# Tile places in SBUF: an identity, two padded buffers and a smaller constant in a one-core encoder kernel

## The chip, the core and the metric

The kernel runs on one core of a Trainium2 chip. TensorE (PE in the profile, with its weight loads as PEld) multiplies, VectorE (DVE), ScalarE (ACT) and GpSimd (POOL) do the elementwise work, and SyncE (SP) issues most transfers. Each engine works through its own list of instructions and waits for the others through semaphores. Operands lie in SBUF, a memory of 128 partitions; a tile has the same byte address in every partition. Products are written to PSUM. The metric is the device time of one execution in microseconds (us).

## What is computed

One layer of a hybrid encoder over 1024 positions of 1024 channels, all in float32:

```python
h = layer_norm(x, emb_ln_g, emb_ln_b)
proj = h @ w_in
q, k, v, z_a, u, z_b, g_a, g_b = split(proj)
attn = neighbourhood_attention(q, k, v, rpb)          # 8 heads of 64
y_a = attn * silu(z_a)
u = centred_depthwise_conv(u, conv_w, conv_b)         # 4 taps
hh = rg_lru(u, gates of direction 0) + rg_lru(u, gates of direction 1, reverse=True)
y_b = hh * silu(z_b)
m = sigmoid(g_a + b_merge[0]) * (y_a @ w_ba) + sigmoid(g_b + b_merge[1]) * (y_b @ w_bb)
out = layer_norm(ALPHA * h + m @ w_out, ln_g, ln_b)
```

In `rg_lru` the gates are `sigmoid(x_block @ w_gate + b_gate)`, with blocks of 64 channels, followed by a linear scan along the sequence.

## The kernel before

**Arithmetic.** A float32 operand is split into a high and a low part of the type fp32r, and a product becomes three: high by high, low by high, high by low (`mm3`, whose matmul is line 134). In `PE.matmul(o, a, b)` the operand `a` is stationary (loaded into the array by a weight load of 128 columns) and `b` is moving (streamed through it, up to 512 columns). The projection and the output product use a Strassen-like scheme of seven products of half size.

**Stages.** First the embedding layer norm, transposes of h and the projections of v and of half of q (to about 82 us). Then 17 pairs of output columns, seven products each (`slot` counts them), and between these, hung into the slots by `at(...)`, the recurrent branch: `take_u` copies u into a padded buffer `up`, `conv_stage` forms four taps from it and splits the result into `us`, and `gate_stage` multiplies `us` by the gate weights `gw` and scans. Then attention (about 430 to 532 us), with the products of the LRU branch as filler, and last the merge and the output product with its layer norm.

**Order.** The instructions of every engine run in the order in which the code issues them (a manual schedule is entered before the first load), and semaphores hold back what isn't ready. Only the few instructions on the constants at the head of the function, the identity among them, stand ahead of that schedule.

**Places.** Pools are stacked, some from the bottom of the partition ("left"), some from the top ("right"), and a tile's size is rounded up to 32 bytes. The pool `cst` is the first one on the left; the six tiles in it are, in the order of their allocation, ident (512 bytes), eps_t, eps_z (4 bytes each), smh (240), warm (4) and sm (240). It starts at byte 640, and the pool `hb` with the high and low parts of h follows it, then `wsp` with the weight parts and `hts`. On the right, `ev` ends the region of `lru` at byte 212960; `lru` holds sp, nsp, three small tiles, us0, us1, r, two buffers up, i, two uc, gw high and low, a and two wh.

**The identity** `ident` is built by `make_identity` with two GpSimd instructions, a memset and an affine select. It is the moving operand of every transpose: of gb_row and gb_col (lines 415 and 213), of the layer-norm tiles x (line 272), of the probabilities p (line 1130) and of the row sums (line 1175). The stationary operand is the data that is transposed.

**The gate products** are issued in `gate_stage`, at line 806: for each of four channel blocks t, two directions d, two halves b and two column halves n, a group of two matmuls, `gw` high and low against the same `us`. That makes 64 matmuls of 512 columns. `us` holds the high part in 64 partitions and the low part in the other 64.

**The halved constants** `smh` are 0.5 times all of `sm`, written once in `decay_rates` (line 651). They are read as a bias by `take_zg` (line 702), and only its columns from `SM_BM` (44) on, the sixteen merge biases, are used.

Of the kernel before, what the change touches and what calls it, by code (L numbers as in the profile page):

```python
# [10 lines left out]
F32 = mybir.dt.float32  # L11
F32R = mybir.dt.float32r
AF = mybir.ActivationFunctionType
ALU = mybir.AluOpType

P = 128
S = 1024
# [29 lines left out]
SM_CW, SM_CB, SM_GB, SM_LAM, SM_BM, SM_N = 0, 16, 20, 36, 44, 60  # L47
# [9 lines left out]
def tiled(ap, n):  # L57

    return ap[:, n * HALF:(n + 1) * HALF].rearrange("p (j r c) -> p j r c", r=GR, c=8)


def gridded(ap, n):

    return ap.rearrange("p (r j c) -> p j r c", r=GR, c=8)[:, 4 * n:4 * n + 4]
# [3 lines left out]
def encoder_kernel(ctx, tc, x, gb1, gb, w_qk, w_v, w_s, w_ba, w_bb, w_gate, smalls, bias, w_out, out):  # L68
    nc = tc.nc
    V, A, G, PE, SP = nc.vector, nc.scalar, nc.gpsimd, nc.tensor, nc.sync  # L70

    def pool(name, side="left", **kw):
        return tc.alloc_tile_pool(name=name, bufs=1, side=side, reuse_waits="tile", **kw)
# [5 lines left out]
    cst = pool("cst")  # L79
# [23 lines left out]
    ga_d = dram.tile([NK, P, S], F32, name="ga_d")  # L103
    gb_d = dram.tile([NK, P, S], F32, name="gb_d")

    ident = cst.tile([P, P], F32, name="ident")
    make_identity(nc, ident[:])
    eps_t = cst.tile([P, 1], F32, name="eps_t")
    V.memset(eps_t[:], EPS)
    eps_z = cst.tile([P, 1], F32, name="eps_z")  # L110
    V.memset(eps_z[:], EPS * TWICE * TWICE)
    smh = cst.tile([P, SM_N], F32, name="smh")
    warm = cst.tile([P, 1], F32, name="warm")
    A.activation(warm[:], eps_t[:], AF.Sqrt)
    sm = cst.tile([P, SM_N], F32, name="sm")

# [527 lines left out]
    lru = pool("lru", "right")  # L644
# [3 lines left out]
    lam = sm[:, SM_LAM:SM_LAM + 8]  # L648

    def decay_rates():  # L650
        V.tensor_scalar(smh[:], sm[:], 0.5, None, ALU.mult)
        V.tensor_scalar(t0[:], lam, -1.0, None, ALU.mult)
        V.tensor_tensor(t0[:], lam, t0[:], ALU.min)
        A.activation(t0[:], t0[:], AF.Exp)
        yield
        V.tensor_scalar(t1[:], t0[:], 2.0, None, ALU.add)
        V.reciprocal(t1[:], t1[:])
        V.tensor_tensor(t0[:], t0[:], t1[:], ALU.mult)
        V.tensor_tensor(t1[:], t0[:], t0[:], ALU.mult)
        V.tensor_scalar(t2[:], t1[:], 1.0 / 21.0, 1.0 / 19.0, ALU.mult, ALU.add)  # L660
        yield
        for n in (17, 15, 13, 11, 9, 7, 5, 3, 1):
            V.tensor_tensor(t2[:], t2[:], t1[:], ALU.mult)
            V.tensor_scalar(t2[:], t2[:], 1.0 / n, None, ALU.add)
            if n in (13, 7, 1):
                yield
        V.tensor_tensor(t2[:], t2[:], t0[:], ALU.mult)
        V.tensor_scalar(t0[:], lam, -1.0, 0.0, ALU.mult, ALU.max)
        V.scalar_tensor_tensor(t0[:], t2[:], 2.0, t0[:], ALU.mult, ALU.add)
        V.tensor_scalar(sp[:], t0[:], C_LRU, None, ALU.mult)  # L670
        V.tensor_scalar(nsp[:], t0[:], -C_LRU, None, ALU.mult)
        yield
# [2 lines left out]

    def take_u(m0):
        for m in (m0, m0 + 1):
            up = lru.tile([P, S + 3], F32, tag="up", bufs=2, name=f"up{m}")
            V.memset(up[:, 0:2], 0.0)
            V.memset(up[:, S + 2:S + 3], 0.0)  # L680
            ups[m] = up

        def consume(mi, n, add, o):
            dst = gridded(ups[m0 + mi][:, 2:2 + S], n)
            if add is None:
                A.copy(dst, tiled(o[:], 0))
            else:
                V.tensor_tensor(dst, tiled(add[:], 0), tiled(o[:], 0), ALU.add)
            return []
        return consume  # L690

    def take_zg(dst, m0, name, col=None):

        def consume(mi, n, add, o, c=None):
            c = o if c is None else c
            if add is not None:
                V.tensor_tensor(c[:], add[:], o[:], ALU.add)
            z = ev.tile([P, HALF], F32, tag="z", bufs=5, name=f"{name}{m0}{mi}{n}")

            def squash():  # L700
                bias = {} if col is None else dict(bias=smh[:, col + m0 + mi:col + m0 + mi + 1])
                A.activation(z[:], c[:], AF.Tanh, scale=0.5, **bias)

            def store():
                if col is None:
                    V.scalar_tensor_tensor(z[:], z[:], 1.0, c[:], ALU.add, ALU.mult)
                SP.dma_start(dst[m0 + mi][:, n * HALF:(n + 1) * HALF], z[:])
            return [squash, store]
        return consume
# [233 lines left out]
            load_k(h)  # L943

    def gates_a(j):
        return lambda: take_zg(ga_d, 2 * j, "ga", SM_BM)

    def gates_b(j):
        return lambda: take_zg(gb_d, 2 * j, "gb", SM_BM + 8)

    takes = [take_q, lambda: take_u(0), lambda: take_zg(zb_d, 0, "zb"), lambda: take_zg(za_d, 0, "za"), gates_a(0), gates_a(1),
             lambda: take_u(2), gates_b(0), lambda: take_zg(zb_d, 2, "zb"), gates_a(2), gates_b(1),
             lambda: take_k(0), gates_a(3), lambda: take_k(2), lambda: take_zg(za_d, 2, "za"), gates_b(2), gates_b(3)]
    rates = decay_rates()
    for slot in range(8, 14):
        at(slot, 1, lambda: next(rates))
# [427 lines left out]
    for slot in range(16):  # L1384
        j, n = divmod(slot, 2)
# [234 lines left out]
    for slot in range(16 + len(plan)):  # L1620
        j, n = divmod(slot, 2)
# [142 lines left out]
```

## Time and profile before

| | |
|---|---|
| median of 3 runs | 663.64 us (663.38 to 663.95) |
| the profiled execution's own time | 663.47 us |
| its span, first to last instruction | 661.7 us |
| mean granted TensorE clock | 0.997 |
| matmuls and weight loads | 3119 each |

The profile is of one execution. Its span leaves out 1.77 us around the first and the last instruction. In a row of a group, the number behind "x" is the count, then come the busy time in us, the mean length of one instruction in ns, and the idle time of its engine just before. A matmul's length in the trace is longer than its distance to the next one, since matmuls overlap in the array: a product of 512 columns is shown with 389 ns and the next one starts some 228 ns after it. A view of a tile gives the lowest, median and highest length, and the start of the first and of the last instruction. A row of the timeline begins with the start in us and the length in us of the run of instructions.

### The profile page before, as it was taken

How to read it: one execution, taken by the hardware profiler on the slowest of the kernel's cores; microseconds unless marked ns; L12 is line 12 of the kernel's file. 1: busy time of each engine (PE TensorE's matmuls, PEld its weight loads, DVE VectorE, ACT ScalarE, POOL GpSimd, SP SyncE). 2: the span in 40 equal slices, each digit the busy share in tenths (PEclk: the TensorE clock that was granted, in tenths of full speed). 3: DMA queues.
4: the chain of work that ended last, by engine and by line, in shares of the span. 5: the costliest groups of instructions: out<-in, count | busy, mean ns of one | idle time of the engine just before them, and what ended most of it. 6: DMA issues, size and time to landing. Idle time of an engine off the chain costs nothing.

```text
span 661.7 us, 9467 instructions
## 1 busy us (share of the span) xinstructions
PE 649.3 (98%) x3119; PEld 542.3 (82%) x3119; DVE 524.5 (79%) x860; ACT 388.7 (59%) x686; POOL 395.6 (60%) x311
## 2 busy tenths in 40 slices
PE   8999999999999999999999999999999999999994
PEld 6888888888888888888788888889888888888883
DVE  7978767986899599879987697177887876994776
ACT  5564433356786677777666834277777734573242
POOL 6799263434676476658556455012552649989857
PEclk9999999999999999999999999999999999999998
DMA  8747607133334133532361548898977288333023
GB/s 326 275 140 247 192 33 230 42 113 125 128 115 140 48 112 108 180 109 83 132 218 60 191 161 286 302 350 272 355 267 243 66 307 295 111 115 127 24 104 128
DMA packets 52481, 113.42 MB, mean 171 GB/s; under 512 B 5504, under 2 KB 9936, under 8 KB 50896
## 3 DMA queue, kind: packets, MB, share of 16 engines
q1 hardware_dynamic: 51968, 112.28, 49.0%
q8 instruction: 25, 0.41, 0.3%
q10 hardware_dynamic: 464, 0.53, 0.2%
q14 instruction: 24, 0.20, 0.1%
HBM read 77.11 MB, written 35.68 MB: 170 GB/s over the span
## 4 chain that ended last, share of the span: by engine, by line
PE 87%; DVE 7%; POOL 2%; issue 1%; ACT 1%; DMA 0%; POOLq 0%; SPq 0%; DVEq 0%; ACTq 0%
PE a L134 32%; PE mb L134 13%; PE s L134 12%; PE x L134 6%; PE w L134 5%; PE v L328 4%; PE acc L1156 3%; PE s L1108 3%; PE pt L1130 3%; PE q L134 2%; PE g L806 2%; POOL x L261 1%; DVE ws_l L128 1%; PE tp L272 1%; DVE uc L764 1%
## 5 line engine op out<-in xcount | busy, mean ns | idle before, releaser
L134 PE MATMUL a<-ht_h,ws_h 128*128 128x512 f32 x136 | 53.1, 391 | 0.0
L134 PE MATMUL a<-ht_h,ws_l 128*128 128x512 f32 x136 | 53.0, 389 | 0.0
L134 PE MATMUL a<-b_h,wa_l 128*128 128x512 f32 x136 | 53.0, 389 | 0.0
L134 PE MATMUL a<-ht_l,ws_h 128*128 128x512 f32 x136 | 52.9, 389 | 0.0
L134 PE MATMUL a<-b_h,wa_h 128*128 128x512 f32 x136 | 52.9, 389 | 0.0
L134 PE MATMUL a<-b_l,wa_h 128*128 128x512 f32 x136 | 52.9, 389 | 0.0
L1118 DVE CUSTOM_DVE_ANT_0 sc<-s,bias 128x384 f32<-128x384 f32 (+1 forms) x64 | 33.4, 523 | 20.2 <-PE s L1108 9.1
L1137 ACT CAST pt_h<-pt 128x384 fp32r<-128x384 f32 x64 | 29.0, 453 | 23.8 <-PE pt L1130 19.3
L1123 ACT ACTIVATE p<-sc,summ 128x384 f32<-128x384 f32 (+1 forms) x64 | 37.9, 592 | 5.5 <-DVE summ L1118 5.1
L134 PE MATMUL mb<-ya,wb_h 128*128 128x512 f32 x128 | 39.7, 390 | 0.0
L914 POOL CAST wb_h<-wb 128x512 fp32r<-128x512 f32 x9 | 7.0, 779 | 48.2 <-DMA wb<-in_w_bb_dram 30.4
L128 DVE TENSOR_TENSOR pt_l<-pt,pt_h 128x384 fp32r<-128x384 f32 x64 | 33.2, 519 | 1.9 <-ACT pt_h L1137 1.5
L328 PE MATMUL v<-wv,b_h 128*128 128x512 f32 x128 | 32.6, 397 | 0.4 <-ACT b_h L427 0.4
L128 POOL TENSOR_TENSOR ht_l<-t,ht_h 128x512 fp32r<-128x512 f32 x16 | 22.0, 1407 | 18.3 <-ACT ht_h L314 18.3
L1522 POOL TENSOR_TENSOR z<-z,gb 128x512 f32<-128x512 f32 (+2 forms) x23 | 27.6, 1215 | 8.6 <-ACT z L1517 7.7
L1108 PE MATMUL s<-ks,qs 128*128 128x384 f32 (+1 forms) x128 | 31.6, 328 | 0.0
L134 PEld LDWEIGHTS a<-ht_h,ws_h 128*128 128x128 f32 x136 | 25.5, 188 | 5.9 <-issue 0.4
L1130 PEld LDWEIGHTS pt<-ident,p 128*128 128x128 f32 x176 | 23.2, 140 | 8.5
L134 PEld LDWEIGHTS a<-b_h,wa_h 128*128 128x128 f32 x136 | 25.5, 188 | 5.4
L134 PEld LDWEIGHTS a<-ht_l,ws_h 128*128 128x128 f32 x136 | 25.5, 188 | 5.4
L134 PEld LDWEIGHTS a<-b_h,wa_l 128*128 128x128 f32 x136 | 25.5, 188 | 5.3
L134 PEld LDWEIGHTS a<-b_l,wa_h 128*128 128x128 f32 x136 | 25.5, 188 | 5.3
(542 smaller groups left out, 2259.4 us busy)
## 6 DMA issues: line engine op xcount, KB each, us to landing
ks<-k_d SPq DMA_DIRECT2D x8, 1024.0 KB, 8.4
h_d<-x SPq DMA_DIRECT2D x8, 512.0 KB, 2.9
v_d<-vs SPq DMA_DIRECT2D x8, 512.0 KB, 3.2
q_d<-q SPq DMA_DIRECT2D x8, 512.0 KB, 3.2
ga_d<-ga SPq DMA_DIRECT2D x16, 256.0 KB, 2.1
gb_d<-gb SPq DMA_DIRECT2D x16, 256.0 KB, 2.5
k_d<-k SPq DMA_DIRECT2D x8, 512.0 KB, 4.0
qs<-q_d SPq DMA_DIRECT2D x8, 512.0 KB, 4.6
```

Source lines behind the costliest of these rows:

```text
L128: eng.tensor_tensor(lo, full, hi.bitcast(F32), ALU.subtract)
L134: PE.matmul(o, a, b, start=first and i == 0, stop=last and i == len(prods) - 1, skip_group_check=not (first and last))
L328: PE.matmul(vos[i][:], a, wv[kind == "w"][k][:], start=vn[i] == 0, stop=vn[i] == 23)
L806: PE.matmul(o[:, n, :], w[:, 2 * d + b, :], us[b][:, n * HALF:(n + 1) * HALF], start=z == 0, stop=z == 1)
L914: G.tensor_copy(hi[:], st[:])
L1108: PE.matmul(o[:, :P * len(near(t))], q[:, t * P:(t + 1) * P], k[:, z, keys], start=z == 0, stop=z == 1)
L1118: V.tensor_tensor_reduce(s[:, :w], o[:, :w], heads[h][2][:, b0:b0 + w], -1.0, 3.0e38, ALU.add, ALU.min, accum_out=sums[h][0][:, t:t + 1])
L1123: A.activation(probs[h % 2][t][:], scs.pop((h, t))[:, :w], AF.Exp, bias=sums[h][0][:, t:t + 1], scale=-1.0, accum_out=sums[h][1][:, t:t + 1])
L1130: PE.transpose(tp[:, n * P:(n + 1) * P], probs[h % 2][t][:, z * P:(z + 1) * P], ident[:])
L1137: A.copy(pt[0][:, span(b)], tps[h, b][:, :P * len(near(b))])
L1156: PE.matmul(acc[n][:, lo - n * HALF:hi - n * HALF], vvs[h // 2][:, b, h % 2, :], pt[:, a:a + hi - lo], start=b in (1, 6) and z == 0, stop= ...
L1522: G.tensor_tensor(z, z, gbs[c, n][:, part], (ALU.mult, ALU.add)[c])
```

## The change

Four edits move tiles. The identity is allocated behind eps_t, eps_z and warm; its two instructions are unchanged. The tile smh has 32 columns in place of 60, of which the 16 merge biases are written, and the gates read them from column 0 and 8 on. The buffers up get 1040 columns in place of 1027, of which the same 1027 are used. The list of products and of transfers is the same.

```diff
-    ident = cst.tile([P, P], F32, name="ident")
-    make_identity(nc, ident[:])
     eps_t = cst.tile([P, 1], F32, name="eps_t")
     V.memset(eps_t[:], EPS)
     eps_z = cst.tile([P, 1], F32, name="eps_z")
     V.memset(eps_z[:], EPS * TWICE * TWICE)
-    smh = cst.tile([P, SM_N], F32, name="smh")
     warm = cst.tile([P, 1], F32, name="warm")
+    ident = cst.tile([P, P], F32, name="ident")
+    make_identity(nc, ident[:])
+    smh = cst.tile([P, 32], F32, name="smh")
     A.activation(warm[:], eps_t[:], AF.Sqrt)
     sm = cst.tile([P, SM_N], F32, name="sm")
...
-        V.tensor_scalar(smh[:], sm[:], 0.5, None, ALU.mult)
+        V.tensor_scalar(smh[:, :16], sm[:, SM_BM:SM_BM + 16], 0.5, None, ALU.mult)
...
-            up = lru.tile([P, S + 3], F32, tag="up", bufs=2, name=f"up{m}")
+            up = lru.tile([P, S + 16], F32, tag="up", bufs=2, name=f"up{m}")
...
-        return lambda: take_zg(ga_d, 2 * j, "ga", SM_BM)
+        return lambda: take_zg(ga_d, 2 * j, "ga", 0)
...
-        return lambda: take_zg(gb_d, 2 * j, "gb", SM_BM + 8)
+        return lambda: take_zg(gb_d, 2 * j, "gb", 8)
```

## The prediction, made before the changed kernel was run

> **What bounds the kernel now.** The page comes first: its head, its busy times and its chain of waits.
>
> ```profile
> span 661.7 us, 9467 instructions
> PE 649.3 (98%) x3119; PEld 542.3 (82%) x3119; DVE 524.5 (79%) x860; ACT 388.7 (59%) x686; POOL 395.6 (60%) x311
> PE 87%; DVE 7%; POOL 2%; issue 1%; ACT 1%; DMA 0%; POOLq 0%; SPq 0%; DVEq 0%; ACTq 0%
> ```
>
> TensorE is busy 98% of the span and holds 87% of the chain that ended last, so a nanosecond less per matmul shortens the kernel unless PE then waits for somebody. The view of waits, for PE alone between 97 and 400 us (the gate stages lie there), has one entry; the timeline around it shows its size.
>
> ```profile
> PE a L134 <- DVE w L839: 0.4, 1, 0.4
> ...
> 321.24 0.19 PEld L134 LDWEIGHTS a<-ht_h,wa_h 128*128 128x128 f32 x1 [0.80 <-DVE w L839]
> 321.25 0.50 PE L134 MATMUL a<-ht_h,wa_h 128*128 128x512 f32 x1 [0.38 <-DVE w L839]
> ```
>
> PE stood still 0.38 us there, and its weight load 0.80 us. What PE gains ahead of 321 us could be lost at this place.
>
> **What the change touches.** It moves tiles and narrows one VectorE instruction; no matmul, load or DMA is added or removed. Places are byte addresses within a partition, from the allocation of the kernel before; those after are worked out from tile sizes, each rounded up to 32 bytes. The constants begin at 640, which is 0 modulo 128.
> - Identity: at 640 now. After it: eps_t, eps_z and warm take 32 bytes each, so ident starts at 736, remainder 96. Its partners, p and x, have remainder 96 already.
> - Weights in the left pools: ident ends at 1248, smh (128 bytes) at 1376, sm (256 bytes) at 1632. Before, these constants ended at 1760. Everything behind moves down by exactly 128 bytes, so its remainder stays 96.
> - Gate operands: the two up buffers grow from 4128 to 4160 bytes, 64 in all. The pool is stacked downwards from 212960, so tiles below up move by -64: us0 from 163744 to 163680, us1 from 167840 to 167776, that is from remainder 32 to 96. Their stationary partner gw stays at 196576, remainder 96. The tile r goes from 32 to 96 as well, the two up buffers from 32 and 64 to 96 and 32.
>
> So two kinds of matmul change their pairing: the gate products (moving us) from 32 against 96, and the transposes (moving ident) from 0 against 96, both to 96 against 96. All others had 96 against 96 before and keep it.
>
> **Gate products.** The view of the tile us has these two rows:
>
> ```profile
> L806 PE MATMUL g<-us,gw_h x32: 394/394/394, 142.7 to 362.8; 128*128 128x512 f32 x32
> L806 PE MATMUL g<-us,gw_l x32: 393/394/397, 142.9 to 363.1; 128*128 128x512 f32 x32
> ```
>
> The same tile in four stretches (first and last shown; the columns are stretch, its length, PE busy and count, weight loads, VectorE, ScalarE, granted clock, DMA) has 16 in each:
>
> ```profile
> 142.00:180.00 38.00, 4.38 (x16) 3.00 (x16) 0.00 (x0) 0.00 (x0) 1.00 0.35 118
> ...
> 320.00:364.00 44.00, 4.38 (x16) 3.00 (x16) 0.00 (x0) 0.00 (x0) 1.00 0.44 154
> ```
>
> The timeline shows four of them behind four ordinary products, and what follows:
>
> ```profile
> 141.79 0.39 PE L134 MATMUL a<-b_l,wa_h 128*128 128x512 f32 x1
> ...
> 142.70 0.39 PE L806 MATMUL g<-us,gw_h 128*128 128x512 f32 x1
> ...
> 143.63 0.39 PE L134 MATMUL a<-b_h,wa_h 128*128 128x512 f32 x1
> ```
>
> Four ordinary products, from 141.79 to 142.70, take 0.91 us or 228 ns each; four gate products, from 142.70 to 143.63, take 0.93 us or 233 ns each. Durations say the same: 394 ns, against 389 for ordinary products of that shape:
>
> ```profile
> L134 PE MATMUL a<-b_h,wa_l 128*128 128x512 f32 x136 | 53.0, 389 | 0.0
> ```
>
> The granted clock is 1.00 in those stretches, so it isn't the clock. Is it the place? One comparison speaks for it: us and gw both lie in the upper part of the partition, and so do yb and wb, but those with remainder 96 on both sides. Just before attention begins (422.5 to 428.5 us) they cost the ordinary price:
>
> ```profile
> L134 PE MATMUL mb<-yb_h,wb_h 128*128 128x512 f32 x8 | 3.1, 389 | 0.0
> ```
>
> The same product within attention (438 to 530 us) costs 395 ns, with the same equal remainders:
>
> ```profile
> L134 PE MATMUL mb<-yb_h,wb_h 128*128 128x512 f32 x49 | 19.4, 395 | 0.0
> ```
>
> So about 6 ns can come from something else as well, and the gate products differ in a second way: they come in accumulation groups of two, into one tile of two PSUM banks. The price per gate product is bounded by 0 (the place isn't the cause) and 5 ns (394 less 389). I take 5, since the surcharge stands in every row of them, 393 at least, whatever runs beside. The sum is 64 x 5 ns = 0.32 us. Of it 48 products, 0.24 us, lie ahead of the wait at 321 us; if VectorE doesn't get earlier there, 0.08 us is left. VectorE's work in those stages is itself released by PE's evacuations, so I take the whole.
>
> [...]
>
> **Transposes.** There are 176 of p, 64 of x, 8 of sums and 16 of gb_col, 264 in all. The view of the tile ident (lowest, median and highest duration in ns):
>
> ```profile
> L1130 PE MATMUL pt<-ident,p x176: 270/272/276, 434.9 to 530.1; 128*128 128x128 f32 x176
> L272 PEld LDWEIGHTS tp<-ident,x x64: 138/140/143, 7.5 to 60.5; 128*128 128x128 f32 x64
> L272 PE MATMUL tp<-ident,x x64: 270/272/331, 7.5 to 60.6; 128*128 128x128 f32 x64
> L213 PE MATMUL gps<-ident,gb_col x16: 272/322/417, 4.0 to 6.5; 128*128 128x128 f32 x16
> L1175 PE MATMUL pt<-ident,sums x8: 272/273/273, 438.7 to 525.9; 128*8 128x128 f32 x8
> ```
>
> Here the rows speak against a gain. ident has remainder 0; its partners have 96 (p and x), 32 or 64 (the two buffers of sums), and in gb_col a new one 4 bytes on for each transpose. The medians of the first three partners are 272 and 273, and the lowest of gb_col is 272 too. The timelines of PE and of the weight loads give the distance from one to the next:
>
> ```profile
> 59.88 1.03 PE L272 MATMUL tp<-ident,x 128*128 128x128 f32 x8
> ...
> 59.88 0.79 PEld L272 LDWEIGHTS tp<-ident,x 128*128 128x128 f32 x7
> ...
> 470.32 0.43 PEld L1156 LDWEIGHTS acc<-pt_l,vv 128*128 128x128 f32 x3
> ```
>
> The groups of the weight loads between 470.3 and 470.6 us give the length of one of the last kind (0.4 us for the three together, 190 ns each):
>
> ```profile
> L1156 PEld LDWEIGHTS acc<-pt_l,vv 128*128 128x128 f32 x3 | 0.4, 190 | 0.0
> ```
>
> Eight transposes start (1.03 - 0.27) / 7 = 109 ns apart, and their weight loads (0.79 - 0.14) / 6 = 108 ns apart, a load being 0.14 us long. The loads of vv, with equal remainders and short products, come (0.43 - 0.19) / 2 = 120 ns apart. So an equal place doesn't bring weight loads closer than the transposes have them now.
>
> The nearest cheaper row of that width, among PE's groups within attention:
>
> ```profile
> L1156 PE MATMUL acc<-pt_l,vv 128*128 128x128 f32 x15 | 3.7, 250 | 0.0
> ```
>
> The bounds: a gain of 22 ns each (272 less 250), and a loss of 6 ns each, by the step from 389 to 395. I take 0, by the equal rows of ident.
>
> [...]
>
> **The rest.** These rows are of the tiles smh and up:
>
> ```profile
> L651 DVE TENSOR_SCALAR smh<-sm x1: 184/184/184, 107.6 to 107.6; 128x60 f32<-128x60 f32 x1
> L764 DVE SCALAR_TENSOR_TENSOR uc<-up,sm,uc x12: 1269/1276/1628, 124.9 to 304.9; 128x1024 f32<-128x1024 f32 x12
> ```
>
> Halving 16 columns in place of 60 saves less than 0.184 us once, on VectorE, under PE's products, so nothing on the path; without that cover, at most 0.18. The merge gates read the same values from new columns. The taps alternate between up buffers with remainders 32 and 64 and have one price (1269 to 1276, one 1628 disturbed), so I cost the new places at nothing for VectorE and ScalarE. What hides a loss there is VectorE's room under PE, 661.7 - 524.5 = 137 us of the span; if all twelve taps took 1628 ns, that would be 4.2 us of it. On GpSimd the order of the identity's two instructions stays; VectorE's two memsets were written behind them and now before, but on another queue. No wait is added and no queue reordered.
>
> The sum against the profiled execution: 663.47 us (span 661.7 and 1.77 around it) less 0.32 is 663.15. The median of the three runs is 0.17 above that execution, so I say **663.3 us**.
>
> **Rivals.**
> 1. The transposes profit as the gates do, 5 ns each: 264 x 5 = 1.32, with the gates 1.64 us less, 662.0. For it: a different remainder is all they share with the gates. Against it: the rows of equal duration above. At the far end, 22 ns each, 5.8 us with 0.32 beside, 657.5.
> 2. The surcharge of the gates comes from their groups of two, or is lost at the wait of 321 us: 663.6, nothing changes. For it: yb's 395 with equal places, and the 0.80 us wait. [...]
> 3. Slower: equal starts are the bad case for transposes. [...] At 6 ns each (389 to 395) it is 1.58 less 0.32, 664.9. It outweighs the gates' gain from 1.2 ns per transpose (0.32 / 264) and gets over 0.2% from 6.3. Against it: ordinary products with equal places are the cheap ones.
>
> **Chances and range.** The forecast 0.58; the first rival 0.16, its far end 0.04; the second 0.15; the third 0.07. A measurement of this kernel tells about 0.2% or 1.33 us from no change. Faster by more than that: the far end and some two thirds of the first rival, 0.14. Slower: the greater part of the third rival, 0.05. The same: 0.81. The range goes from 661.7 (first rival) to 664.7 (most of the third, and a run like the highest of before, 663.95).
>
> **What would show it.** Right: g<-us at 389 ns and its stages at 4.29 in place of 4.38 us; pt<-ident and tp<-ident at 272 as now; PE's wait near 321 us not longer. Wrong: gate rows at 394 (second rival), transposes below 267 (first) or from 274 on (third), or any PE idle time that was not there.

## The result, and the profile after

The changed kernel took 666.65 us (median of 6 executions, 666.42 to 667.25), the kernel before 663.36 us (663.20 to 663.95) beside it. The ratio is 1.0049, with a 95% interval from 1.0036 to 1.0062: **slower by 3.3 us or half a per cent**. The forecast was 663.3 us and no change; the range ended at 664.7. Of the eleven executions of the first experiment below, one took 2290 us; it is left out of that run's ratio. The head of the page, its busy times and its chain of waits:

```profile
span 664.7 us, 9466 instructions
PE 652.7 (98%) x3119; PEld 543.0 (82%) x3119; DVE 522.0 (79%) x860; ACT 388.7 (58%) x686; POOL 395.6 (60%) x311
PE 88%; DVE 6%; POOL 2%; issue 1%; ACT 1%; DMA 0%; POOLq 0%; DVEq 0%; ACTq 0%
```

The span is 3.0 us longer and PE is busy 3.4 us more with the same 3119 matmuls. VectorE, ScalarE and GpSimd have no more work than before, and PE's one wait in the projection is 0.3 us where it was 0.4. So single matmuls must be longer, and the chain of waits in order of time shows where. Each row is a run of products on PE: start, length, what, and how many. Before:

```profile
60.91 10.90 PE v L328 x48
71.81 10.88 PE q L134 x48
82.69 8.24 PE a L134 x36
...
401.56 10.88 PE a L134 x48
532.44 43.70 PE mb L134 x192
576.14 10.88 PE x L134 x48
...
638.70 10.89 PE x L134 x48
```

After:

```profile
61.19 11.14 PE v L328 x48
72.33 11.04 PE q L134 x48
83.37 8.23 PE a L134 x36
...
402.18 10.88 PE a L134 x48
533.18 44.62 PE mb L134 x192
577.80 11.19 PE x L134 x48
...
641.48 11.20 PE x L134 x48
```

Read the starts against each other. The lag is 0.28 us at v, 0.52 at q and 0.68 at the first a. Across the whole projection, 319 us of the busiest work, it stays there (0.62 at the last a). It is 0.74 when the merge products mb begin, 1.66 at the first x, 2.78 at the last, and 3.0 at the end. The loss is in the first 83 us and, most of all, in the last 130. Each of these runs is longer by itself: 192 products mb by 0.92 us, 48 products x by 0.31. The groups of PE's matmuls give the price of one. Before:

```profile
L134 PE MATMUL mb<-ya,wb_h 128*128 128x512 f32 x128 | 39.7, 390 | 0.0
...
L134 PE MATMUL x<-b11h,a11l 128*128 128x512 f32 x16 | 6.2, 389 | 0.0
```

After:

```profile
L134 PE MATMUL a<-b_h,wa_l 128*128 128x512 f32 x136 | 52.9, 389 | 0.0
...
L134 PE MATMUL mb<-ya,wb_h 128*128 128x512 f32 x128 | 40.3, 395 | 0.0
...
L134 PE MATMUL x<-b11h,a11l 128*128 128x512 f32 x16 | 6.3, 395 | 0.0
...
L134 PE MATMUL x<-t2h,s2l 128*128 128x512 f32 x16 | 6.2, 389 | 0.0
```

Before, mb of ya cost 390 ns by the high and 389 by the low part of wb, and all products of 512 columns of the output 389. Now mb and x of b11 cost 395, and x of t2h, in the same stage and of the same shape, still 389. What tells these apart is the side of the partition from which they come. In b11h by a11l the moving operand is in a pool on the right and the stationary one in a pool on the left; t2h and s2l both lie on the left. In mb, ya is on the left and wb on the right. In the products a of the projection both are on the left. In the first 83 us part of the products v and q pair left with right as well: wqk, for one, lies on the right, and q of b_h by wqk_l goes from 389 to 393 ns.

**The left pools moved by 128 bytes, the right ones didn't.** Modulo 128 that changes nothing. Modulo 256 it takes the left from remainder 224 to 96, while the right stays at 224. And the gate products, which were meant to gain, are no cheaper. This is the view of the tile us after the change:

```profile
L806 PE MATMUL g<-us,gw_h x32: 392/398/404, 143.4 to 363.5; 128*128 128x512 f32 x32
L806 PE MATMUL g<-us,gw_l x32: 395/395/397, 143.6 to 363.7; 128*128 128x512 f32 x32
```

Their operands are now equal modulo 128 (96), but modulo 256 us has 96 and gw 224. The theory to be tested was that **a product of 512 columns costs some 5 to 6 ns more wherever its two operands differ modulo 256**. The rivals: the identity's new place, the new up buffers, or that left and right moved against each other at all.

Three more groups of the changed kernel show that the theory is too simple for the single product:

```profile
L134 PE MATMUL x<-t3h,s3l 128*128 128x512 f32 x16 | 6.3, 396 | 0.0
L134 PE MATMUL w<-b22h,s4l 128*128 128x512 f32 x16 | 6.3, 395 | 0.0
L134 PE MATMUL w<-b22h,s4h 128*128 128x512 f32 x16 | 6.3, 395 | 0.0
```

All three cost 389 before. b22h and s4l both lie on the right, so their product has equal operands and is dearer all the same; s4h, of the products before and behind it, lies on the left. In twelve of the sixteen x of t3h by s3l both lie on the left. So the price doesn't stay with the unequal pair: products beside one pay it too.

### The profile page after: what moved, and what is told of

Same layout as the page of the kernel before. It is cut to its first block, busy times and chain, and to the rows that moved or that the text cites. A ratio compares the mean times of both kernels' runs of the same rounds, so it can differ in the third digit from the quotient of the medians.

```text
span 664.7 us, 9466 instructions
## 1 busy us (share of the span) xinstructions
PE 652.7 (98%) x3119; PEld 543.0 (82%) x3119; DVE 522.0 (79%) x860; ACT 388.7 (58%) x686; POOL 395.6 (60%) x311
## 4 chain that ended last, share of the span: by engine, by line
PE 88%; DVE 6%; POOL 2%; issue 1%; ACT 1%; DMA 0%; POOLq 0%; DVEq 0%; ACTq 0%
PE a L134 32%; PE mb L134 13%; PE s L134 12%; PE x L134 6%; PE w L134 5%; PE v L328 4%; PE acc L1156 3%; PE s L1108 3%; PE pt L1130 3%; PE q L134 2%; PE g L806 2%; POOL x L261 1%; DVE ws_l L128 1%; PE tp L272 1%; DVE uc L764 1%
```

## The experiments

All times are medians beside the kernel before on the same chip (663.39 us for the first four runs, 663.41 for the last three).

**The identity alone.** smh keeps its 60 columns, so the constants keep their total and every pool its place; the identity goes from 640 to 736, remainder 224 of 256 as p and x have it.

```diff
-    ident = cst.tile([P, P], F32, name="ident")
-    make_identity(nc, ident[:])
...
-    smh = cst.tile([P, SM_N], F32, name="smh")
     warm = cst.tile([P, 1], F32, name="warm")
+    ident = cst.tile([P, P], F32, name="ident")
+    make_identity(nc, ident[:])
+    smh = cst.tile([P, SM_N], F32, name="smh")
```

> The kernel before with the identity alone moved behind eps_t, eps_z and warm (736, remainder 224 of 256, as its partners p and x); all other places are those of before. Theory (a product costs some 5 ns more where its two operands differ modulo 256, and the loss of 3.1 us came from the left pools moving 128 bytes against the right ones): nothing is lost here, 663.2 to 663.5, transposes 272 ns as before; if the identity at a different remainder also cost attention its surcharge (yb by wb 395 instead of 389), some 0.7 us less. Rival (the new place or the later start of the identity cost the 3 us): 666 to 667.

Measured: 663.45 us, ratio 1.0001 (0.9992 to 1.0011). The transposes, by the tile ident, and the products of yb among PE's groups:

```profile
L1130 PE MATMUL pt<-ident,p x176: 270/272/275, 434.8 to 529.8; 128*128 128x128 f32 x176
L272 PE MATMUL tp<-ident,x x64: 270/272/329, 7.4 to 60.5; 128*128 128x128 f32 x64
```

```profile
L134 PE MATMUL mb<-yb_h,wb_h 128*128 128x512 f32 x64 | 25.2, 394 | 0.0
```

The identity costs nothing and brings nothing: 272 ns as before. The surcharge on yb by wb within attention stays as well, so it doesn't come from the identity.

**smh alone.** The identity stays first and up keeps its size; only the left pools move, by 128 bytes. The merge gates read smh from column 0 and 8 on, as in the changed kernel.

```diff
-    smh = cst.tile([P, SM_N], F32, name="smh")
+    smh = cst.tile([P, 32], F32, name="smh")
...
-        V.tensor_scalar(smh[:], sm[:], 0.5, None, ALU.mult)
+        V.tensor_scalar(smh[:, :16], sm[:, SM_BM:SM_BM + 16], 0.5, None, ALU.mult)
...
```

> The kernel before with smh alone narrowed to 32 columns: every left pool moves by 128 bytes, the identity and up stay. Theory (equality modulo 256): the whole loss is here, 666.2 to 667.0, with mb by ya 395 ns instead of 390 and the output products 393 to 395 instead of 389, gates unchanged at 394. Rival (equality modulo 128 is what matters, and the loss came from up or the identity): 663.2 to 663.5.

Measured: 667.45 us, ratio 1.0063 (1.0050 to 1.0076). Among PE's groups:

```profile
L134 PE MATMUL mb<-ya,wb_h 128*128 128x512 f32 x128 | 40.4, 396 | 0.0
...
L134 PE MATMUL x<-b11h,a11l 128*128 128x512 f32 x16 | 6.3, 395 | 0.0
```

The whole loss is here, with the product prices that the theory asked for, and 0.45 us more than the upper end of the expectation. The gates were not "unchanged": the products by gw_h cost 398 (394 before), those by gw_l 394, though us and gw kept their places. Only the operands on the left of the products around them had moved, another sign that neighbours pay.

**The left pools by another 128 bytes.** From the changed kernel, smh is dropped and the biases are halved in place in sm. Left and right then stand 256 bytes farther apart than before, and are equal again modulo 256. The merge gates read sm from column SM_BM and SM_BM + 8 on.

```diff
-    smh = cst.tile([P, 32], F32, name="smh")
...
-        V.tensor_scalar(smh[:, :16], sm[:, SM_BM:SM_BM + 16], 0.5, None, ALU.mult)
+        V.tensor_scalar(sm[:, SM_BM:SM_BM + 16], sm[:, SM_BM:SM_BM + 16], 0.5, None, ALU.mult)
...
-                bias = {} if col is None else dict(bias=smh[:, col + m0 + mi:col + m0 + mi + 1])
+                bias = {} if col is None else dict(bias=sm[:, col + m0 + mi:col + m0 + mi + 1])
...
```

> The changed kernel with the biases halved in place in sm and no smh, which moves the left pools by another 128 bytes, 256 in all from before; up keeps its 1040 columns, so us has remainder 96 and gw 224 of 256 (equal modulo 128). Theory: left and right are equal modulo 256 again, so mb by ya back to 389 to 390 and the output products to 389; gates stay at 394 to 398; 663.0 to 663.6. Rival 1 (distance itself or the other edits cost): 666 to 667. Rival 2 (equality modulo 128 decides for the gates): gates 389.

Measured: 662.97 us, ratio 0.9994 (0.9985 to 1.0002). One line of code is gone, so lines behind it count one less. PE's groups:

```profile
L133 PE MATMUL mb<-ya,wb_h 128*128 128x512 f32 x128 | 39.6, 389 | 0.0
...
L133 PE MATMUL x<-b11h,a11l 128*128 128x512 f32 x16 | 6.2, 389 | 0.0
```

The loss is gone, with the identity and up in their new places. That the pools moved against each other isn't the cause; by how much they differ modulo 256 is. The gates, equal modulo 128 alone, are not at 389 throughout, but those by gw_l come below the expected 394, at a median of 390 (the tile us):

```profile
L805 PE MATMUL g<-us,gw_h x32: 395/396/398, 142.7 to 362.6; 128*128 128x512 f32 x32
L805 PE MATMUL g<-us,gw_l x32: 387/390/397, 142.9 to 362.8; 128*128 128x512 f32 x32
```

**The gates equal modulo 256 too.** As the run above, with wider up buffers, which put us at 163552, remainder 224 as gw.

```diff
-            up = lru.tile([P, S + 16], F32, tag="up", bufs=2, name=f"up{m}")
+            up = lru.tile([P, S + 32], F32, tag="up", bufs=2, name=f"up{m}")
```

> As the run with the left pools moved by 256, and up with 1056 columns, so that us also has remainder 224 of 256 as gw has. Theory: gates 389 ns, 64 x 5 = 0.3 us less than that run, 662.6 to 663.3, the fastest of the four. Rival (the gates' surcharge comes from their groups of two): gates 394 to 398 as before, time equal to that run.

Measured: 662.66 us, ratio 0.9990 (0.9981 to 0.9999), the fastest kernel of the study. The tile us:

```profile
L805 PE MATMUL g<-us,gw_h x32: 389/389/390, 142.7 to 362.3; 128*128 128x512 f32 x32
L805 PE MATMUL g<-us,gw_l x32: 388/389/389, 142.9 to 362.6; 128*128 128x512 f32 x32
```

The same groups of two into the same two PSUM banks cost 389 ns once the places agree. So groups of two are not the cause. From the run above 32 products gain 7 ns (396 to 389) and 32 gain 1, which is 0.26 us; the medians differ by 0.31, less than single executions of one kernel scatter (662.78 to 663.29 us in the run above), so the rows show this gain better than the times. The chains of waits of the two kernels show that the gain gets through the wait near 321 us. First the run above, then this one:

```profile
280.69 8.17 PE a L133 x36
321.12 5.74 PE a L133 x24
...
401.33 10.88 PE a L133 x48
```

```profile
280.54 8.17 PE a L133 x36
320.94 5.73 PE a L133 x24
...
401.02 10.88 PE a L133 x48
```

0.15 us ahead of the wait, 0.18 behind it, 0.31 at the end of the projection.

**Three smaller distances.** smh with 52, 44 and 36 columns moves the left pools by 32, 64 and 96 bytes; the rest is as with smh alone. The question was whether the price grows with the distance.

```diff
-    smh = cst.tile([P, SM_N], F32, name="smh")
+    smh = cst.tile([P, 52], F32, name="smh")
```

> smh with 52 columns, so the left pools move by 32 bytes against the right ones (192 against 224 of 256); all else as in the run with smh alone. Theory A (any difference costs the full price): mb by ya 395 ns, 666 to 667.5. Theory B (the price grows with the distance, here a quarter of 128): mb by ya 390 to 391, 663.9 to 664.6. Theory C (only some distances hurt): 663.2 to 663.6.

> smh with 44 columns: the left pools move by 64 bytes (160 against 224). us keeps 160 and gw 224, so gates stay at 394. Theory A: mb by ya 395 ns, 666 to 667.5. Theory B (half of the price at 128): 392 to 393, 664.6 to 665.6. Theory C: 663.2 to 663.6.

> smh with 36 columns: the left pools move by 96 bytes (128 against 224); the identity stays at 128 of 256 and now has the same remainder as its partners p and x. Theory A: mb by ya 395 ns, 666 to 667.5. Theory B (three quarters): 393 to 394, 665.6 to 666.6. Either way transposes at 272 ns as in all runs so far.

Measured: 667.52 us (ratio 1.0061, 1.0046 to 1.0076), 667.43 (1.0059, 1.0044 to 1.0074) and 667.49 (1.0061, 1.0044 to 1.0077). The group of mb with 32 and with 96 bytes:

```profile
L134 PE MATMUL mb<-ya,wb_h 128*128 128x512 f32 x128 | 40.4, 395 | 0.0
```

```profile
L134 PE MATMUL mb<-ya,wb_h 128*128 128x512 f32 x128 | 40.5, 396 | 0.0
```

Theory A holds for the time and for mb (the first lies 0.02 us above its range): 32 bytes cost as much as 128 (667.52 and 667.45 us). A quarter of the price at a quarter of the distance would have been 663.9 to 664.6. Single groups are less regular: at 64 bytes x of b11l by a11h, left by right, costs 389 ns, and x of t2h by s2h, both on the left, 395. The gates, expected at 394 there, come at 398 and 392.

## Why the prediction was wrong, point by point

- **What bounds the kernel** was right. PE is the chain, and a few nanoseconds on each of some 500 matmuls came out as microseconds at the end.
- **The step that failed** is in "What the change touches": the left pools "move down by exactly 128 bytes, so its remainder stays 96", and with it "All others had 96 against 96 before and keep it". The arithmetic was right and the modulus wrong. The remainder that counts is that of 256: the products of left by right went from 389 to about 395 ns, which the prediction had put at nothing, and with the left pools alone moved the kernel took 667.45 us. The trace of before couldn't show it, since it held no pair of this kind 128 bytes apart: its only unequal products of 512 columns, us by gw, were 64 apart (160 and 224), which is unequal by either modulus. But then 128 was an assumption, and nothing in the trace bore it out; a rival with a larger modulus, priced at 6 ns for each of the 464 products of left by right, would by this estimate have given 2.8 of the 3.3 us (464 x 6 ns).
- **Gate products.** The cause was right (place, not groups of two) and so was the size: 5 ns predicted, 394 before and 389 in the run with all equal, where the 32 by gw_h and the 32 by gw_l take 12.4 us each (12.6 before). But the change didn't make them equal. At 128 apart they cost 398 and 395.
- **The wait at 321 us** doesn't swallow the gain, as forecast: in the run with all equal 0.15 us stand before it and 0.18 behind it.
- **Transposes** at no gain: right, a median of 272 ns for p and of 272 or 273 for x in every run, with the identity 32, 64, 96 or 128 bytes away from p or at the same remainder.
- **The rest** at nothing: right. Taps after the change, from the tile up:

```profile
L764 DVE SCALAR_TENSOR_TENSOR uc<-up,sm,uc x12: 1272/1276/1628, 124.1 to 305.6; 128x1024 f32<-128x1024 f32 x12
```

- **The rivals.** None was it. The third had the right sign and the wrong products: it put the loss on the transposes and on equal places, and the loss is on the 512-column products and on unequal ones. Its own time, 664.9, also lay outside the range that was to cover most of it. The second put the surcharge of the gates down to their groups of two, and that doesn't agree with the runs: between the third and the fourth experiment only the width of up and the places below it differ, and the gate products go from 396 and 390 to 389.

What stands behind it in the chip is not shown. The runs show that the loss comes and goes with the remainders modulo 256: 667.45 us with the left pools alone moved by 128 bytes, 662.97 with 256. They don't give a rule for the single product. In the trace of before a load of gw_l and the product by gw_h ahead of it both start at 142.70 us, and that product lasts 0.39, so weights are loaded while the product before still runs. It stays open whether the places of a moving operand and its own weights count or those of the next ones; after the change b22h by s4l has the first equal, b22h by s4h the second, and both cost 395. What is shown at 389 throughout is an output stage in which all places agree, before and in the third and the fourth experiment.

## What to carry to other kernels

Where TensorE is the bound and weights change with every matmul, as here, look at the addresses of moving and stationary operands modulo 256, not only at shapes: 32 bytes less in a pool of constants cost this kernel 4 us (663.41 to 667.52). Edits that seem to be about one small tile move every pool stacked on it, so list the remainders of all pairs before and after, those from opposite ends of the partition above all. And when a prediction rests on a rule with a number in it, look whether the trace holds a case that tells that number from its double.

## What the runs showed of the hardware

- In the merge and the output stage, products of 128 by 512 in fp32r cost 389 to 390 ns in the trace when all places there are equal modulo 256. When left and right differ, the groups of left by right cost mostly 392 to 399, and some groups of equal products among them up to 396. The distances 32, 64, 96 and 128 are alike in the time of the kernel, 667.4 to 667.5 us with only the left pools moved. A distance of 256 is as cheap as 0 (ya 34528 and wb 204768, remainders 224 and 480 of 512, in the kernel before: 389 to 390 ns).
- Transposes of p and x by the identity are not touched by it: a median of 272 ns for p and of 272 or 273 for x at every distance tried.
- The products of yb by wb within attention cost 394 ns on the mean even with everything equal, where the kernel before had 389 for them outside attention. That surcharge has another cause, which was not looked for.
- The kernels with the identity in its old place and moved left pools (667.4 to 667.5 us) are 0.8 us slower than the changed kernel (666.65), at nearly the same price per product (mb of ya by the high part of wb 395 to 396 ns against 395). In the profiled execution with smh alone the first sixteen transposes take 3.62 us where the changed kernel takes 2.88 and before 2.74. With 64 bytes they take 2.61, and that execution, 666.8 us, is the fastest of its kernel. With smh alone all sixteen start (3.62 - 0.42) / 15 = 213 ns apart; before, the first nine do (4.01 to 5.71 us), and the others follow some 109 apart. But the start can't be the whole: with 96 bytes they take only 2.4 us, and that execution takes 667.58. Where the rest lies, and whether places have to do with it, stays open.
